# The opening stages of an encoder block: engine order written out, tiles cast one ahead, sums evacuated one late, every second stage backwards

## The chip, the cores and the metric

The kernel runs on one core of one Trainium2 chip. The metric is the device time of one execution in microseconds (us). Before the change the median of three runs was 1933.44 us (1930.73 to 1934.36). About 0.2% (4 us) is what a measurement of this kernel can tell from no change.

## The reference, cut to what matters

One layer over a sequence of 256 tokens with 2048 channels, all in float32: a feed-forward half-step, a mixer of two recurrent kinds of heads, and a second feed-forward half-step. Each of the three sublayers reads `x` normalised and then scaled and shifted by a vector that is computed from a conditioning vector `c` ("adaLN"). The change lies in the first sublayer.

```python
mod = (jax.nn.silu(c) @ w_ada + b_ada).reshape(B, 3, 3, D_MODEL)
shift, scale, gate = mod[:, :, 0], mod[:, :, 1], mod[:, :, 2]
def modulate(h, s):
    return _layer_norm(h) * (1.0 + scale[:, s]) + shift[:, s]
g, v = jnp.split(modulate(x, 0) @ w13, 2, axis=-1)      # 2048 x 2*5632
y = (jax.nn.silu(g) * v) @ w2                           # 5632 x 2048
x = _layer_norm(ALPHA * x + 0.5 * gate[:, 0] * y, ln_g, ln_b)
```

## The kernel before, in words

**Products.** Every float32 product is made of three fast ones: an operand is split into a rounded high part and the rest, and high x high, high x low and low x high are summed in PSUM. For a weight tile of 128x2048 that means one load (SyncE's queue), one rounding copy on ScalarE into `hi` (L93) and one subtraction on VectorE into `lo` (L95); `load_w` (L98) does the three. The tiles `raw` have four buffers in all, `hi` and `lo` three each.

**The adaLN vectors.** Each tile of `w_ada` (1 MB, same `raw` buffers) gives 128 elements of a shift, scale or gate vector: VectorE multiplies it by the row of silu(c), which stands in all partitions (`scb`), and sums along it (`ada_tile`, L167). A fraction of such a tile rides along with each weight tile: `tick` (L184) adds a rate to a credit and issues one adaLN tile per whole credit. `ada_until` (L179) issues what is needed now.

**The ramp** (`ramp`, L646). The first 24 blocks of 128 hidden channels of the first sublayer are computed in five stages over the 16 channel blocks of the input (`STAGES` = 2, 3, 3, 4, 4), so that TensorE can start as soon as two adaLN pairs are known. In each stage the loops run over b = 0..5 and p = 0, 1 (gate or value half): twelve pairs (b, p). A pair has two sums of 128 tokens x 512 columns, one PSUM bank each, and 6 products for each channel block of the stage, 1152 in all. The banks are eight. The pair b = 3 keeps its four banks through all stages (`KEPT`); the others are added to a running sum in SBUF after each stage (L726 to L732: in stage 0 copies, most on ScalarE and some on VectorE, then VectorE adds). Before the last pair or the last but one of a stage, `modulate` (L206) prepares the next stage: transposes on TensorE, scale and shift on ScalarE (L217), rounding (L220), the rest on VectorE (L221); `ahead` is the next stage's first weight tile. In stage 0 the pairs of `EARLY` begin with channel block 0 alone.

**What sets the order.** Where code calls an engine through `V`, `A`, `G`, `T` (L123, `Pinned`), its instructions stay in program order among themselves. All others (`nc.vector`, `nc.scalar`, `nc.tensor`, `nc.sync`) are put in an order by the framework's scheduler, which also gives a new tile whichever buffer comes free. In the ramp before, nearly all casts, sums and evacuations are of the second kind; only the opening (`A.copy`, `V.tensor_sub` in L691 to L700) is pinned. After the ramp `g2(0)` (L760) follows with products `py`.

Of the kernel before, what the change touches and what calls it, by code (L numbers as in the profile page):

```python
# [16 lines left out]
P = 128  # L17
# [32 lines left out]
def block_kernel(ctx: ExitStack, tc: tile.TileContext, a: dict, out: bass.AP):  # L50
# [35 lines left out]
    def split(tile, act, low):  # L86

        raw, name, into = tile
        hi, lo = into() if into else [wp.tile([P, 2048], F32R, tag=w, bufs=3, name=w[0] + name) for w in ("hi", "lo")]
        step = 512 if fine[0] else 2048  # L90
        cols = [slice(c, c + step) for c in range(0, 2048, step)]
        for w in cols:
            act.copy(cut(hi, w), like(raw[:, w], hi))  # L93
        for w in cols:
            low.tensor_sub(cut(lo, w), like(raw[:, w], lo), cut(hi, w).bitcast(F32))  # L95
# [68 lines left out]

    todo = list(enumerate(_ada_tiles()))

    def ada_tile(vec=nc.vector, parts=1):  # L167
        i, (s, j, kt) = todo.pop(0)
        raw = raw_tile(f"ada{i}")
        nc.sync.dma_start(raw, a["w_ada"][i])  # L170
        base = badac[:, s, j, kt:kt + 1]
        for n in range(parts):
            c = slice(n * D // parts, (n + 1) * D // parts)

            to = adac[:, s, j, kt:kt + 1] if n == parts - 1 else sc[:, n:n + 1]
            vec.tensor_tensor_reduce(raw[:, c], raw[:, c], scb[:, c], 1.0, base, ALU.mult, ALU.add, to)  # L176
            base = to

    def ada_until(s, j, kt):  # L179

# [25 lines left out]
    def modulate(s, ns, k0, k, act=nc.scalar, vec=nc.vector):  # L206

        for kt in range(k0, k0 + k, 2):
            w = min(2, k0 + k - kt)
            ps = bank(f"tu{s}_{kt}")  # L210
            for j in range(w):
                for t in range(NT):
                    nc.tensor.transpose(ps[:, j * S + t * P:j * S + (t + 1) * P],
                                        ns[t][:, (kt + j) * P:(kt + j + 1) * P], ident)
            u = sm.tile([P, 2, S], F32, tag="u", bufs=2, name=f"u{s}_{kt}")
            for j in range(w):
                act.activation(u[:, j, :], ps[:, j * S:(j + 1) * S], AF.Identity,  # L217
                                     bias=modc[:, s, 0, kt + j:kt + j + 1],
                                     scale=modc[:, s, 1, kt + j:kt + j + 1])
            act.copy(uh[:, kt:kt + w, :], u[:, 0:w, :])  # L220
            vec.tensor_sub(ul[:, kt:kt + w, :], u[:, 0:w, :], uh[:, kt:kt + w, :].bitcast(F32))  # L221
# [357 lines left out]
    def ffn(s, w13, w2, start, following=None):  # L579
# [65 lines left out]

        def ramp(ns):  # L646

            kept = {}
            n_w = k0 = 0
            ns, rest = ns()  # L650
            for st, k in enumerate(STAGES):
# [5 lines left out]
                held = {}  # L657
                hls = {} if first else {0: ahead}

                def tile_of(i):  # L660
                    if i not in hls:
                        hls[i] = load_w(a["w13_r"][n_w + i], f"ra{n_w + i}")
                    return hls[i]

                def banks(b, p):
                    if b == KEPT:
                        if first:
                            kept[p] = [bank(f"k{'gv'[p]}{t}") for t in range(NT)]
                        return kept[p]
                    return [bank(f"r{'gv'[p]}{st}_{b}{t}") for t in range(NT)]  # L670

                def products(b, p, pss, j0, j1):

                    for t in range(NT):
                        tk = slice(t * P, (t + 1) * P)
                        for j in range(j0, j1):
                            i = (2 * b + p) * k + j
                            hi, lo = tile_of(i // 4)
                            w = slice(i % 4 * 512, (i % 4 + 1) * 512)
                            go = j == 0 and (first or b != KEPT)  # L680
                            end = j == k - 1 and (last or b != KEPT)
                            nc.tensor.matmul(pss[t], uh[:, k0 + j, tk], hi[:, w], start=go, stop=False)
                            nc.tensor.matmul(pss[t], uh[:, k0 + j, tk], lo[:, w], start=False, stop=False)  # L683
                            mm = nc.tensor.matmul(pss[t], ul[:, k0 + j, tk], hi[:, w], start=False, stop=end)  # L684
                    return mm

                if first:


                    credit[1] = 0.0  # L690
                    ada_tile(V, 2)  # L691
                    ada_tile(V)
                    raw, _, _ = load(a["w13_r"][0], "ra0")
                    hi, lo = hls[0] = [wp.tile([P, 2048], F32R, tag=w, bufs=3, name=w[0] + "ra0") for w in ("hi", "lo")]
                    for i in (0, 2, 1, 3):
                        w = slice(i * 512, (i + 1) * 512)
                        A.copy(hi[:, w], raw[:, w])
                        V.tensor_sub(lo[:, w], raw[:, w], hi[:, w].bitcast(F32))
                        if i == 0:
                            modulate(0, ns, 0, 1, A, V)  # L700
                    for n, (b, p) in enumerate(EARLY):
                        held[b, p] = banks(b, p)
                        products(b, p, held[b, p], 0, 1)
                        if n == 0:
                            rest()
                    with tc.issue_after(V.last.ins):
                        ada_until(0, 1, 1)
                    credit[:] = 0.0, RAMP_RATE[0]
                    modulate(0, ns, 1, 1)
                for b in range(RAMP // 4):  # L710
                    for p in range(2):

                        if b == RAMP // 4 - 1 and p == (k > 2) and not last:
                            k1 = k0 + k
                            tile_of(3 * k - 1)
                            ahead = load_w(a["w13_r"][n_w + 3 * k], f"ra{n_w + 3 * k}")
                            ada_until(0, 1, k1 + STAGES[st + 1] - 1)
                            modulate(0, ns, k1, STAGES[st + 1])
                        if (b, p) in held:
                            pss = held[b, p]  # L720
                            end = products(b, p, pss, 1, k)
                        else:
                            pss = banks(b, p)
                            end = products(b, p, pss, 0, k)
                        if b != KEPT:
                            for t in range(NT):  # L726
                                if first and p and t:
                                    nc.vector.tensor_copy(part[b, p][t], pss[t])
                                elif first:
                                    nc.scalar.copy(part[b, p][t], pss[t])  # L730
                                else:
                                    nc.vector.tensor_add(part[b, p][t], part[b, p][t], pss[t])  # L732
                        turn_one(end)
                    if last and b < 4:
                        g, v = (kept if b == KEPT else {p: part[b, p] for p in range(2)}).values()
                        for t in range(NT):
                            swiglu(b, t, g[t], v[t])
                n_w += 3 * k
                k0 += k

        def g1(gi):
            grp = groups[gi]
# [461 lines left out]
def _layout(x, c, w_ada, b_ada, ffn1_w13, ffn1_w2, w_in, b_in, mlstm_norm_g, rg_conv_w, rg_conv_b, rg_wa, rg_ba,  # L1204
# [5 lines left out]
    o["w_ada"] = np.stack([w[t] for t in _ada_tiles()])  # L1210
    o["b_ada"] = _chan(b_ada[0])
    for i, (w13, w2) in enumerate(((ffn1_w13, ffn1_w2), (ffn2_w13, ffn2_w2)), 1):

# [4 lines left out]

    w = ffn1_w13[0].reshape(KT, P, 2, NFF // 4, 512)[:, :, :, :RAMP // 4]
    k0, tiles = 0, []  # L1220
    for k in STAGES:
        tiles.append(w[k0:k0 + k].transpose(1, 3, 2, 0, 4).reshape(P, -1, 2048).transpose(1, 0, 2))
        k0 += k
    o["w13_r"] = np.ascontiguousarray(np.concatenate(tiles))
    w, b = w_in[0], b_in[0]
# [37 lines left out]
```

## Time and profile before

| | |
|---|---|
| Median of three runs | 1933.44 us (1930.73 to 1934.36) |
| The profiled execution, its own time | 1936.85 us |
| Its span from first to last instruction | 1934.9 us |
| TensorE busy | 1892.8 us, 98% of the span |
| VectorE, ScalarE busy | 1429.8 us (74%), 841.1 us (43%) |
| Moved from HBM | 509.22 MB, 264 GB/s over the span |

In the views, PE is TensorE's matmuls, PEld its weight loads, DVE VectorE, ACT ScalarE, POOL GpSimd, SP SyncE (SPq: its DMA issues). PEclk is the clock that TensorE was granted, as a share of full speed. A name such as `rra` is the raw weight tile of the ramp, `hra` and `lra` its two parts; `rg` and `rv` the sums for gate and value half, `kg` and `kv` those that keep their banks; `yacc`, `gate` and `x` are the places in SBUF where the others are added up; `tu` the transposed input, `u` the modulated one; `ada` a tile of `w_ada`. A matmul's record lasts longer than its spacing, since they are pipelined. Lines that begin with a start time are from a timeline: start, duration, engine, line, operation; in brackets the idle time before it and what ended that.

### The profile page before, as it was taken

Reading aid. Unit: us, or ns where it says so; the run is one execution under the profiler, and the core shown is the slowest. Engines: PE = TensorE matmul, PEld = TensorE weight load, DVE = VectorE, ACT = ScalarE, POOL = GpSimd, SP = SyncE. Lnnn points to the kernel's source line nnn. Section 1 sums busy time; section 2 is a strip of 40 time slices with the busy share of each in tenths; the row PEclk is TensorE's granted clock in tenths of the full one; section 3 lists DMA queues with packets and bytes.
Section 4 is the critical chain, followed back from the end, with each engine's and each line's share of the span. In section 5 each row is a group of like instructions: output and inputs, shape, how many; then the busy total and the mean of one; then the engine's idle time right before and its main releaser. Section 6 shows DMA issues by size and latency. Waiting matters only on the chain.

```text
span 1934.9 us, 21428 instructions
## 1 busy us (share of the span) xinstructions
PE 1892.8 (98%) x8680; PEld 1562.4 (81%) x8680; DVE 1429.8 (74%) x1381; ACT 841.1 (43%) x808; POOL 35.3 (2%) x59
## 2 busy tenths in 40 slices
PE   6999999999999999999999999999999999999997
PEld 5878788888888888788888886888888888888885
DVE  7999898887877988798987886655656644445656
ACT  5434344533334335757543346533444334333350
POOL 0000000000000000000000121000000000000000
PEclk8999999999999999999999999999999999999999
DMA  8998878998888787477787674666666655554562
GB/s 349 350 345 328 324 284 328 348 347 323 325 318 334 293 338 287 147 292 263 255 310 283 229 290 177 239 225 254 246 253 250 230 194 196 187 187 177 191 226 77
DMA packets 72675, 512.71 MB, mean 265 GB/s; under 512 B 8448, under 2 KB 8576, under 8 KB 10880
## 3 DMA queue, kind: packets, MB, share of 16 engines
q1 hardware_dynamic: 70848, 507.54, 70.4%
q10 hardware_dynamic: 1728, 3.80, 0.5%
q8 instruction: 68, 1.11, 0.2%
q14 instruction: 31, 0.25, 0.0%
HBM read 509.22 MB, written 2.10 MB: 264 GB/s over the span
## 4 chain that ended last, share of the span: by engine, by line
PE 89%; DVE 5%; issue 3%; DMA 2%; ACT 1%; POOL 0%; DVEq 0%; ACTq 0%; POOLq 0%
PE pj L249 6%; PE py L259 6%; PE py L261 6%; PE py L260 6%; PE fg L259 6%; PE fg L261 6%; PE fg L260 6%; PE fv L260 6%; PE fv L261 6%; PE fv L259 6%; PE pj L250 3%; PE tl L260 2%; PE tl L261 2%; PE tl L259 2%; PE rg L683 2%
## 5 line engine op out<-in xcount | busy, mean ns | idle before, releaser
L176 DVE CUSTOM_DVE_ANT_0 ada<-ada,scb,badac 128x2048 f32<-128x2048 f32 x142 | 333.5, 2351 | 60.1 <-DMA ada<-in_w_ada 59.8
L95 DVE TENSOR_TENSOR lw<-rw,hw 128x2048 fp32r<-128x2048 f32 x80 | 183.3, 2291 | 107.5 <-ACT hw L93 107.5
L93 ACT CAST hw<-rw 128x2048 fp32r<-128x2048 f32 x80 | 153.1, 1914 | 242.6 <-PE py L261 119.7
L95 DVE TENSOR_TENSOR lfv<-rfv,hfv 128x2048 fp32r<-128x2048 f32 x60 | 137.5, 2292 | 129.3 <-ACT hfv L93 129.3
L95 DVE TENSOR_TENSOR lfg<-rfg,hfg 128x2048 fp32r<-128x2048 f32 x60 | 137.5, 2291 | 97.2 <-ACT hfg L93 97.2
L93 ACT CAST hfg<-rfg 128x2048 fp32r<-128x2048 f32 x60 | 114.9, 1915 | 198.1 <-PE fv L261 74.1
L259 PE MATMUL py<-hw,hth 128*128 128x512 f32 x512 | 200.1, 392 | 0.0
L261 PE MATMUL py<-hw,htl 128*128 128x512 f32 x512 | 199.4, 389 | 0.0
L260 PE MATMUL py<-lw,hth 128*128 128x512 f32 x512 | 199.1, 389 | 0.0
L93 ACT CAST hfv<-rfv 128x2048 fp32r<-128x2048 f32 x60 | 114.8, 1913 | 179.8 <-PE fg L261 137.3
L259 PE MATMUL fg<-hfg,u 128*128 128x512 f32 x480 | 187.8, 392 | 0.0
L261 PE MATMUL fg<-hfg,u 128*128 128x512 f32 x480 | 186.9, 389 | 0.0
L260 PE MATMUL fv<-lfv,u 128*128 128x512 f32 x480 | 186.7, 389 | 0.0
L261 PE MATMUL fv<-hfv,u 128*128 128x512 f32 x480 | 186.7, 389 | 0.0
L260 PE MATMUL fg<-lfg,u 128*128 128x512 f32 x480 | 186.7, 389 | 0.0
L259 PE MATMUL fv<-hfv,u 128*128 128x512 f32 x480 | 186.6, 389 | 0.0
L249 PE MATMUL pj<-u,hs 128*128 128x512 f32 x512 | 181.3, 399 | 0.0
L93 ACT CAST hra<-rra 128x2048 fp32r<-128x2048 f32 x47 | 89.9, 1914 | 136.5 <-PE rv L684 48.9
L250 PE MATMUL pj<-u,ls 128*128 128x256 f32 x512 | 143.8, 281 | 0.0
L249 PEld LDWEIGHTS pj<-u,hs 128*128 128x128 f32 x512 | 96.1, 188 | 23.4
L95 DVE TENSOR_TENSOR lra<-rra,hra 128x2048 fp32r<-128x2048 f32 x47 | 107.4, 2287 | 7.9 <-ACT hra L93 7.9
L261 PEld LDWEIGHTS py<-hw,htl 128*128 128x128 f32 x512 | 96.1, 188 | 20.2
(449 smaller groups left out, 3593.0 us busy)
## 6 DMA issues: line engine op xcount, KB each, us to landing
ada<-in_w_ada SPq DMA_DIRECT2D x144, 1024.0 KB, 5.0
rw<-in_w SPq DMA_DIRECT2D x80, 1024.0 KB, 4.9
rfg<-in_w SPq DMA_DIRECT2D x60, 1024.0 KB, 4.9
rfv<-in_w SPq DMA_DIRECT2D x60, 1024.0 KB, 4.9
rra<-in_w_r SPq DMA_DIRECT2D x48, 1024.0 KB, 5.7
rs<-in_w_s SPq DMA_DIRECT2D x32, 1024.0 KB, 5.0
rwo<-in_w_out SPq DMA_DIRECT2D x16, 1024.0 KB, 4.8
rv<-in_w_vo SPq DMA_DIRECT2D x8, 1024.0 KB, 4.8
```

The lines of the kernel that those rows point to most:

```text
L93: act.copy(cut(hi, w), like(raw[:, w], hi))
L95: low.tensor_sub(cut(lo, w), like(raw[:, w], lo), cut(hi, w).bitcast(F32))
L176: vec.tensor_tensor_reduce(raw[:, c], raw[:, c], scb[:, c], 1.0, base, ALU.mult, ALU.add, to)
L249: nc.tensor.matmul(ps, hi[:, w], u2[:, k].rearrange("p w b -> p (w b)"), start=k == 0, stop=False)
L250: nc.tensor.matmul(ps[:, 0:S], lo[:, w], uh[:, k, :], start=False, stop=k == KT - 1)
L259: nc.tensor.matmul(o, acth[:, k0 + j, tk], cut(hi, w), start=first and j == 0, stop=False)
L260: nc.tensor.matmul(o, acth[:, k0 + j, tk], cut(lo, w), start=False, stop=False)
L261: end = nc.tensor.matmul(o, actl[:, k0 + j, tk], cut(hi, w), start=False, stop=last and j == 3)
L683: nc.tensor.matmul(pss[t], uh[:, k0 + j, tk], lo[:, w], start=False, stop=False)
```

## The change

Five things change, all of them in the ramp.

- The ramp's tiles are cast by `A` and `V`, in program order, and adaLN sums go to `V` (`ordered`). At each pair the casts are issued for the tile that it needs and one tile more.
- A pair's sums are evacuated during the next pair (`pending`, `evacuate`), the first time by a ScalarE copy, later by a VectorE add.
- The pairs of every second stage run backwards (`_pairs`), and the last pair of a stage, which is the first of the next, keeps its banks (`carried`). The weight tiles in HBM are laid out in this order (`_pieces`).
- The opening is written out (`first_stage`): the first adaLN tile (a shift) is stored transposed and summed by TensorE, 16 products with one column each; the first tiles are loaded in halves, and the first weight tile's first quarter ahead of the scale; three pairs begin with channel block 0 instead of two.
- The rates at which adaLN tiles ride along change in stages 0 to 2.

```diff
-EARLY = ((0, 0), (0, 1))
-
-RAMP_RATE = (1.0, 0.67, 0.89, 0.67, 0.75)
+EARLY = ((0, 0), (0, 1), (1, 0))
+def _pairs(st):
+    out = [(b, p) for b in range(RAMP // 4) for p in range(2)]
+    return out[::-1] if st % 2 else out
+def _pieces(st):
+    head = [(*e, j) for j in range(STAGES[st]) for e in EARLY] if st == 0 else []
+    return head + [(b, p, j) for b, p in _pairs(st) for j in range(STAGES[st]) if (b, p, j) not in head]
+RAMP_RATE = (1.5, 0.78, 0.78, 0.67, 0.75)
...
+    ordered = [nc.scalar, nc.vector]
...
-        return split(load(src, name, into), nc.scalar, nc.vector)
+        return split(load(src, name, into), *ordered)
...
+    def ada_tile():
+        for _ in ada_sum(ada_load(), ordered[1]):
+            pass
...
+            ordered[:] = A, V
...
+            def evacuate():
+                if not pending:
+                    return
+                b, p, pss, to_h = pending.pop()
+                if b != KEPT:
+                    for t in range(NT):
+                        if (b, p) in written:
+                            V.tensor_add(part[b, p][t], part[b, p][t], pss[t])
+                        else:
+                            A.copy(part[b, p][t], pss[t])
+                    written.add((b, p))
...
+            def first_stage(ps, tile_of, products, banks, hls, held):
+                shift = ada_load(2)
+                raw = raw_tile("rra0")
+                nc.sync.dma_start(raw[:, 0:512], a["w13_r"][0, :, 0:512])
+                scale = ada_load(2)
+                nc.sync.dma_start(raw[:, 512:], a["w13_r"][0, :, 512:])
+                more = [ada_load(2) for _ in range(2)]
...
+                pa = bank("pa")
+                for kt in range(KT):
+                    T.matmul(pa[:, 0:1], shift[0][:, kt * P:(kt + 1) * P], sc[:, kt:kt + 1],
+                             start=kt == 0, stop=kt == KT - 1)
...
+                for _ in ada_sum(scale, V, 2):
+                    pass
+                high(0)
+                A.activation(adac[:, 0, 0, 0:1], pa[:, 0:1], AF.Identity, bias=badac[:, 0, 0, 0:1])
+                u_low = u_of(0)
+                low(0)
+                u_low()
+                for i in (1, 2, 3):
+                    high(i)
+                steps = chain(*(ada_sum(t, V, 2) for t in more))
+                low(1)
+                next(steps)
+                low(2)
+                for _ in steps:
+                    pass
+                for b, p in EARLY:
+                    held[b, p] = banks(b, p)
+                    products(b, p, held[b, p], 0, 1)
+                u_low = u_of(1)
+                low(3)
+                u_low()
...
+                tile_of(1)
+                fine[0] = False
+                credit[:] = -RAMP_RATE[0], RAMP_RATE[0]
+                tile_of(2)
+                rest()
...
+                    goes_on = not first and (b == KEPT or (b, p) == pairs[0])
+                    stays = not last and (b == KEPT or (b, p) == pairs[-1])
...
+                for b, p in pairs:
+                    need = max(pieces.index((b, p, j)) for j in range(k)) // 4
+                    for i in range(min(need + 2, n_tiles)):
+                        tile_of(i)
+                    if need == n_tiles - 1 and not new_u:
+
+                        ahead = load_w(a["w13_r"][n_w + n_tiles], f"ra{n_w + n_tiles}")
+                        evacuate()
+                        for kt in range(k0 + k, k0 + k + STAGES[st + 1], 2):
+                            w = min(2, k0 + k + STAGES[st + 1] - kt)
+                            ada_until(0, 1, kt + w - 1)
+                            modulate(0, ns, kt, w, A, V)
+                        new_u = True
+                    evacuate()
...
+                    if not last and (b, p) == pairs[-1]:
+                        carried = (b, p), pss
+                    else:
+                        pending.append((b, p, pss, last and b < 4))
+                    turn_one(end)
```

More of the change, by code (lines that the diff above doesn't have):

```diff
@@ L646, in ramp @@
         def ramp(ns):
-            kept = {}
+            kept, written, pending, carried = {}, set(), [], None
             n_w = k0 = 0
+            ordered[:] = A, V
             ns, rest = ns()
+            ahead = None
+            def evacuate():
[9 more added lines that the diff above has]
+                    written.add((b, p))
+                if to_h and p:
+                    g, v = (kept if b == KEPT else {p: part[b, p] for p in range(2)}).values()
+                    for t in range(NT):
+                        swiglu(b, t, g[t], v[t])
@@ L656, in ramp @@
                     new_h(1)
-                held = {}
+                pairs, pieces, n_tiles = _pairs(st), _pieces(st), 3 * k
+                held = {} if first else {carried[0]: carried[1]}
                 hls = {} if first else {0: ahead}
@@ L676, in products @@
                         for j in range(j0, j1):
-                            i = (2 * b + p) * k + j
+                            i = pieces.index((b, p, j))
                             hi, lo = tile_of(i // 4)
                             w = slice(i % 4 * 512, (i % 4 + 1) * 512)
-                            go = j == 0 and (first or b != KEPT)
-                            end = j == k - 1 and (last or b != KEPT)
+                            go = j == 0 and not goes_on
+                            end = j == k - 1 and not stays
                             nc.tensor.matmul(pss[t], uh[:, k0 + j, tk], hi[:, w], start=go, stop=False)
@@ L687, in ramp @@
                 if first:
[L690 to L737, printed above, removed]
@@ L738, in ramp @@
-                n_w += 3 * k
+                    first_stage(bank("tu0"), tile_of, products, banks, hls, held)
+                new_u = last
+                for b, p in pairs:
[11 more added lines that the diff above has]
+                    evacuate()
+                    if (b, p) in held:
+                        pss = held[b, p]
+                        end = products(b, p, pss, 1 if first else 0, k)
+                    else:
+                        pss = banks(b, p)
+                        end = products(b, p, pss, 0, k)
+                    if not last and (b, p) == pairs[-1]:
+                        carried = (b, p), pss
+                    else:
+                        pending.append((b, p, pss, last and b < 4))
+                    turn_one(end)
@@ L1220, in _layout @@
     k0, tiles = 0, []
-    for k in STAGES:
-        tiles.append(w[k0:k0 + k].transpose(1, 3, 2, 0, 4).reshape(P, -1, 2048).transpose(1, 0, 2))
+    for st, k in enumerate(STAGES):
+        tiles.append(np.stack([w[k0 + j, :, p, b] for b, p, j in _pieces(st)]).reshape(-1, 4, P, 512).transpose(
+            0, 2, 1, 3).reshape(-1, P, 2048))
         k0 += k
```

37 lines of the change are left out of this document (32 added, 5 removed).

## The prediction, made before the changed kernel ran

> **What bounds the kernel now.** I read the page first: who is busy, and at what clock.
>
> ```profile
> PE 1892.8 (98%) x8680; PEld 1562.4 (81%) x8680; DVE 1429.8 (74%) x1381; ACT 841.1 (43%) x808; POOL 35.3 (2%) x59
> PE   6999999999999999999999999999999999999997
> PEclk8999999999999999999999999999999999999999
> ```
>
> TensorE sets the time; only the first slice shows a gap and a lower clock. So I cut the ramp where TensorE's idle times lie (windows view; columns: window, its length, busy time of PE, PEld, DVE, ACT, POOL with counts, granted clock, DMA share, GB/s).
>
> ```profile
> 18.79:24.53 5.74, 5.73 (x14) 4.12 (x14) 5.64 (x7) 5.07 (x5) 0.00 (x0) 0.53 0.97 405
> 24.53:26.89 2.36, 0.01 (x1) 0.01 (x1) 2.36 (x3) 0.97 (x2) 0.00 (x0) 1.00 0.99 399
> 26.89:34.47 7.58, 5.53 (x16) 4.09 (x16) 4.40 (x6) 3.46 (x4) 0.00 (x0) 0.77 0.89 369
> 34.47:37.62 3.15, 3.15 (x7) 2.48 (x8) 2.22 (x2) 0.61 (x2) 0.00 (x0) 0.50 0.66 218
> 37.62:59.04 21.42, 20.75 (x93) 16.68 (x91) 17.20 (x13) 12.66 (x15) 0.00 (x0) 0.99 0.91 357
> 107.40:125.16 17.76, 15.68 (x71) 12.12 (x69) 17.50 (x17) 7.92 (x8) 0.00 (x0) 1.00 0.85 325
> 125.16:227.67 102.51, 102.38 (x454) 84.27 (x455) 93.75 (x82) 37.24 (x24) 0.00 (x0) 1.00 0.89 334
> 227.67:236.05 8.38, 5.43 (x21) 4.27 (x20) 8.38 (x7) 4.76 (x7) 0.00 (x0) 0.80 0.78 271
> 307.66:1934.90 1627.24, 1607.40 (x7433) 1328.97 (x7431) 1152.58 (x1121) 707.60 (x682) 33.00 (x48) 0.99 0.68 253
> ```
>
> Ramp and 1152 products lie between 18.79 and 307.66 us. TensorE idles there for 0.01 + 2.35 + 2.05 + 0.67 = 5.1 us up to 59.04 and 2.08 + 0.13 + 2.95 = 5.2 us later. Half clock costs more: length times missing clock is 2.7 + 1.7 + 1.6 + 0.2 = 6.2 us up to 59.04 and 0.20 x 8.38 = 1.7 us at 228 to 236. So 18 us can be had in the ramp. Behind it TensorE works 1607.40 of 1627.24 us: what the ramp gives or loses reaches the end nearly whole. The waits name the places:
>
> ```profile
> PE rg L682 <- ACT u L118: 4.3, 1, 4.3
> PE rv L682 <- ACT u L217: 3.0, 1, 3.0
> PE rg L682 <- ACT u L220: 2.4, 1, 2.4
> PE rg L683 <- DVE lra L95: 2.1, 1, 2.1
> PE rg L682 <- DVE yacc L732: 1.1, 1, 1.1
> PE rv L682 <- DVE x L732: 0.9, 1, 0.9
> PE rg L682 <- ACT u L217: 0.7, 1, 0.7
> ```
>
> The first is the wait for the first product. The second, third and last are waits for a modulated input, 2.1 us one for a low part, and 1.1 + 0.9 us waits for a bank that VectorE had still to empty.
>
> **Prices.** Timelines give spacings, which count where work queues up:
>
> ```profile
> 299.73 0.39 PE L683 MATMUL rg<-lra,u 128*128 128x512 f32 x1
> 307.43 0.39 PE L684 MATMUL rv<-hra,u 128*128 128x512 f32 x1
> 226.17 2.35 DVE L176 CUSTOM_DVE_ANT_0 ada<-ada,scb,badac 128x2048 f32<-128x2048 f32 x1 [1.91 <-DMA ada<-in_w_ada]
> 228.45 2.29 DVE L95 TENSOR_TENSOR lra<-rra,hra 128x2048 fp32r<-128x2048 f32 x1
> 230.65 1.28 DVE L732 TENSOR_TENSOR x<-x,rg 128x512 f32<-128x512 f32 x2
> 231.85 2.28 DVE L95 TENSOR_TENSOR lra<-rra,hra 128x2048 fp32r<-128x2048 f32 x1
> 227.82 0.71 PE L213 MATMUL tu<-ident,n 128*128 128x128 f32 x5
> L213 PE MATMUL tu<-ident,n x32: 270/272/473, 11.5 to 228.3; 128*128 128x128 f32 x32
> ```
>
> Between the two products lie 34 steps (33 products stand between them): 7.70 / 34 = 0.2265 us each. A low part takes VectorE 230.65 - 228.45 = 2.20 us, an adaLN sum 2.28 with its read-out, an add 1.20 / 2 = 0.60, and five transposes whose single records last 0.27 at the least are over in 0.71: (0.71 - 0.27) / 4 = 0.11 us each.
>
> **Part 1, the opening and stage 0.** Before, the first product hangs on the first weight tile:
>
> ```profile
> 5.40 6.25 PE L142 MATMUL pc<-ident,sc 128*128 128x128 f32 x32 [5.40 <-ACT sc L149]
> 13.83 1.28 DVE L118 CUSTOM_DVE_ANT_0 ada<-ada,scb,sc 128x1024 f32<-128x1024 f32 x1
> 17.22 0.62 ACT L118 CAST hra<-rra 128x512 fp32r<-128x512 f32 x1 [3.27 <-DMA rra<-in_w_r]
> 17.75 0.56 ACT L118 ACTIVATE u<-tu,adac 128x256 f32<-128x256 f32 x1
> 18.79 0.79 PE L682 MATMUL rg<-hra,u 128*128 128x512 f32 x1 [4.32 <-ACT u L118]
> 6.56:9.79 3.23, 3.23 (x17) 3.23 (x16) 3.19 (x7) 1.19 (x3) 0.23 (x1) 1.00 0.97 389
> 10.30:13.71 3.41, 1.46 (x12) 1.23 (x11) 2.99 (x6) 2.61 (x7) 0.86 (x3) 1.00 1.01 425
> 12.27:17.24 4.97, 0.47 (x1) 0.18 (x1) 4.72 (x5) 1.03 (x5) 0.63 (x2) 0.67 1.01 427
> DMA to landing us min/median/max: 4.8/6.2/12.2
> ```
>
> The weight tile is the fifth megabyte on the queue (two of `x`, two adaLN tiles, itself) and lands at 17.2 at 427 GB/s, 2.46 us for each (the last row is the ramp's weight loads, issue to landing: at least 4.8 us). In the new order the scale ends after 4.25 MB, so at 15.4; its second half is summed by 16.7. TensorE's half: the shift's halves land at 11.0 and 12.3. Sixteen float32 products are 32 records, as `pc` shows; at `pc`'s 6.25 / 32 = 0.195 us they end at 11.65 + 6.25 = 17.9, at the 1.46 / 12 = 0.12 us of the window at full clock at 12.3 + 16 x 0.12 = 14.2. That clock held until 13.7, so I take some 18 of them fast and 14 slow: 16.5, and with four transposes 17.4; `u` needs both this and the scale. From the start of `u` to the first product it is 1.04 us as now: 18.4 (17.8 to 19.8). Next late is channel block 1: ScalarE's quarter cast, then on VectorE two quarters at 0.6 and four half sums at 1.28, then `u`: 18.4 + 0.5 + 6.3 + 1.0 = 26.2. The 18 early products (4.1 us of work) fill 7.8 us, whatever the clock: 3.7 lost. From there 126 products need 28.5 us and up to 1.7 for a slow start: 56.4. VectorE's list from 26.2 is 1.0 + 2.4 (tile 1) + 5 x 2.20 + 6 adaLN x 2.28 = 28.1: 54.3 without any wait, and now in fixed order. It will wait for casts, which ScalarE issues behind `rest()` and 18 copies. I take stage 1's first product at 60. Now: at 59.04 TensorE had done 40.25 - 11.3 = 28.9 of stage 0's 144 x 0.2265 + 1.1 = 33.7 us, so the same point stands at 63.9. **-3.9 us**, with ends -7.5 (56.4) and +0.5. The upper end is this: if tile 1 gets the first weight tile's buffer and not the scale's, its load waits for the last quarter's subtraction at 26.8, lands 4.8 us later and costs some 4.4 us.
>
> The loads in halves put more issues on SP's queue, where the transfers (427 GB/s, back to back) and not the issues are the limit; if halves run like `x`'s 512 KB pieces (389 GB/s), the scale lands 0.5 us later, inside the ends. The Trainium skill speaks against halves: "DMA: Bandwidth & Descriptors", Bandwidth, wants transfers of at least 1 MiB and gives 341 GB/s for a 1 MB transfer. At no more than that the scale's sum would come 1.4 us later (an estimate), 0.7 us past TensorE's half, and the forecast would be 1924.9; in the trace pieces of 512 KB that queue up ran at 389.
>
> **Part 2, stages 1 and 2.** VectorE's work in stage 2 was 9 x 2.20 + 8 adaLN (0.89 x 9) x 2.28 + 20 x 0.60 + 1.2 = 51.2 us against TensorE's 216 x 0.2265 + 0.9 = 49.8: hence full VectorE and lost 2.08 + 0.13 us at 107 to 168. Now 7 sums (0.78 x 9) and 18 adds, since the carried pair isn't evacuated: 19.8 + 16.0 + 10.8 + 1.2 = 47.8. Stage 1, which gets the seventh sum and has 16 adds (one pair's first copies fall to ScalarE): 46.6 against 49.6. Both fit. **-2.2 us** (0 to -2.2); next late would be TensorE itself.
>
> **Part 3, the end of stage 3.** Here `u` waited:
>
> ```profile
> 227.69 1.91 ACT L93 CAST hra<-rra 128x2048 fp32r<-128x2048 f32 x1 [3.53 <-PE rg L684]
> 229.51 1.92 ACT L217 ACTIVATE u<-tu,adac 128x256 f32<-128x256 f32 x4
> 231.48 0.47 PE L682 MATMUL rv<-hra,u 128*128 128x512 f32 x1 [2.95 <-ACT u L217]
> ```
>
> `rv` is the last pair of stage 3. Kept banks 4, the pair before 2, `tu` 2: it waits until `u` empties a `tu` bank, and `u` stands behind a cast that itself waited for TensorE to free a `hi` buffer. Cast one ahead, that cast has its buffer a pair earlier (a pair is a tile here, 24 products, 5.4 us). So `u` starts with the transposes, and the pair's banks come from two adds. **-4.6 us** (2.95 idle and 1.7 of half clock; 0 if the add stands behind another 2.2 us instruction). The Trainium skill, "TensorE: Matmul & The Clock Gate", Why this matters for your kernels, has idle gaps up to about 3 us keep the clock. By that the term is -2.95 and the forecast 1925.9; the trace disagrees: after 2.36 and 2.95 us of idle the clock fell to 0.77 and 0.80.
>
> **Part 4, what the fixed order adds.** VectorE's add for a pair now stands behind the next tile's adaLN sum and low part, ScalarE's copies and `u` behind a cast; behind a waiting instruction queue all later ones, and TensorE waits for banks. The trace of before has no such order. Nearest rows: a boundary or bank wait that is not the big one costs 0.7 to 1.1 us. Bounds: 0, and 4.6 at each of four boundaries, 18.4. I take **+1.5**, two such waits, because a pair lasts 4.1 us or more and the add needs 1.2.
>
> Layout and reversal remove and add no product and no byte: nothing. Sum: -3.9 - 2.2 - 4.6 + 1.5 = -9.2. The profiled execution took 1936.85 us, 3.41 above the median of the runs: 1927.65 there, **1924.2** as a median.
>
> **Rivals.** *A, slower: VectorE's order.* Slack for each tile is (49.6 - 46.6) / 9 = 0.33 us in stage 1, 0.22 in stage 2, 0.79 in stage 3 (12 tiles; 288 x 0.2265 + 0.9 = 66.1 against 26.4 + 8 x 2.28 + 18 x 0.60 + 1.2 = 56.6) and 0.21 in stage 4 (65.2 + 32 transposes = 68.7 against 26.4 + 18.2 + 20 adds and 16 steps of the gated product at 0.60 = 66.2). If each low part waits w for its cast with the adds behind it, stages 1, 2 and 4 lose 30 w - 7.5 us. From w = 0.53 that eats the 8.5 us of parts 1 and 3; at 0.8 it is 16.5, and the time 1933.4 - 8.5 + 16.5 = 1941. For it: VectorE was full. Against:
>
> ```profile
> DVE lra L95 <- ACT hra L93: 7.9, 6, 2.7
> ```
>
> 7.9 us over 47 tiles is 0.17 each, and ScalarE has room.
>
> *B, no change:* stage 0 at its late end (+0.5), `u` still late at the end of stage 3, only part 2 left: -1.7, 1931.7. For it: `u` still stands behind `ahead`'s cast in program order. *C, half:* as B in stage 0, but part 3 holds: 0.5 - 2.2 - 4.6 + 1.5 = -4.8, 1928.6.
>
> **Numbers.** Forecast 0.58, C 0.17, B 0.13, A 0.12. Within 0.2% (4 us, what a measurement of this kernel can tell) are B and a good third of C: 0.20; slower 0.12; faster 0.68. Range: below, parts 1 to 3 at their best and part 4 nil, -14.3: 1919; above, past C and B to 1934, leaving out most of A.
>
> **What would show it.** First product near 18.4; stage 1's near 60; no wait of PE for L732 near 107 to 125; no gap of 3 us near 225 and clock 1.00 from about 40 us on; `py` from about 298.5 instead of 307.66. Wrong if VectorE's waits for `hra` pass 20 us, or PE waits for adds at stage ends.

## The result, and the profile after

| | before | after |
|---|---|---|
| Median | 1932.09 us (1930.63 to 1934.36, 4 runs) | 1962.73 us (1961.66 to 1965.35, 4 runs) |
| Profiled execution, its span | 1936.85 us, 1934.9 us | 1965.35 us, 1963.2 us |

The ratio is 1.0159, interval 1.0146 to 1.0172: slower by some 30 us, where 9.2 us less was forecast. One execution of `e1_evac_first`, a kernel of the experiments below, took 2463.41 us at a granted clock of 0.727; that kernel's figures leave it out. The page of the changed kernel, to be set against the first rows of the prediction (busy time; TensorE and its clock in 40 slices of 49 us):

```profile
PE 1905.3 (97%) x8712; PEld 1570.8 (80%) x8712; DVE 1422.3 (72%) x1373; ACT 844.5 (43%) x817; POOL 35.3 (2%) x59
PE   7899988999999999999999999999999999999997
PEclk8999998999999999999999999999999999999998
```

The first slice is better than before (7 for 6). The second (49 to 98 us), the sixth and the seventh (245 to 344 us) stand at 8 where all were 9, and in the seventh the clock dips too. Cut at the gaps (windows view of the changed kernel; columns as in the prediction, PE's busy time second):

```profile
18.21:53.80 35.59, 32.17 (x126) 24.92 (x126) 28.30 (x29) 22.44 (x29) 0.00 (x0) 0.91 0.94 357
53.80:60.08 6.28, 0.01 (x2) 0.00 (x1) 5.13 (x6) 2.44 (x3) 0.00 (x0) 0.87 0.95 382
60.08:109.06 48.98, 48.98 (x204) 39.98 (x204) 40.66 (x34) 20.20 (x18) 0.00 (x0) 0.95 0.84 322
109.06:114.22 5.16, 1.03 (x6) 0.62 (x6) 4.32 (x5) 2.84 (x4) 0.00 (x0) 0.89 0.94 357
114.22:166.10 51.88, 51.88 (x216) 42.38 (x216) 43.69 (x40) 16.80 (x11) 0.00 (x0) 0.94 0.76 282
166.10:171.57 5.47, 1.29 (x10) 0.84 (x9) 4.36 (x5) 2.84 (x4) 0.00 (x0) 0.96 0.97 367
171.57:268.00 96.43, 96.43 (x425) 79.77 (x426) 80.47 (x70) 37.40 (x29) 0.00 (x0) 0.98 0.79 296
268.00:330.00 62.00, 50.50 (x210) 39.29 (x208) 43.52 (x44) 22.80 (x23) 0.00 (x0) 0.89 0.55 208
329.43:1963.20 1633.77, 1611.93 (x7455) 1332.05 (x7453) 1163.81 (x1133) 709.30 (x683) 32.98 (x48) 1.00 0.69 255
```

Idle time plus length times missing clock, counted as the prediction did for before:

| Stretch | idle | half clock | lost |
|---|---|---|---|
| opening and most of stage 0 (to 53.80) | 3.4 | 0.09 x 35.59 = 3.2 | 6.6 |
| before stage 0's last two pairs | 6.3 | 0.05 x 48.98 = 2.4 | 8.7 |
| before stage 1's last two pairs | 4.1 | 0.06 x 51.88 = 3.1 | 7.2 |
| before stage 2's last two pairs | 4.2 | 0.02 x 96.43 = 1.9 | 6.1 |
| last stage | 11.5 | 0.11 x 62.00 = 6.8 | 18.3 |

With a wait of 1.6 us just behind them this is 48.5 us; before it was 18.2 (5.1 + 5.2 idle, 6.2 + 1.7 clock). The difference is 30.3. The ramp grew by 28.9 (the spans' 28.3, and its first product came 0.58 earlier), which is the same as nearly as a clock of two digits allows. Behind the ramp nothing changed: of the last row's 1633.77 us, 22 records of the ramp (5.0) and the 1.6 are still the ramp's, and 1627.2 are left, as before. So the ramp lost it all, and the last stage most. What ended TensorE's waits (18 to 337 us):

```profile
PE rg L796 <- ACT x L135: 6.3, 1, 6.3
PE rg L796 <- ACT u L135: 5.6, 3, 3.6
PE rg L797 <- DVE lra L135: 3.7, 2, 2.7
PE rv L796 <- ACT u L135: 3.6, 1, 3.6
PE kv L797 <- DVE lra L135: 2.7, 1, 2.7
PE kv L796 <- ACT hra L135: 2.2, 1, 2.2
PE rg L796 <- ACT hra L135: 2.0, 1, 2.0
```

ScalarE's evacuating copies (`x`) and its `u` hold the boundaries; in the last stage casts and low parts do. Those two engines have time to spare (busy 43% and 72%), so the next question is what they stood at. VectorE's waits in the same stretch, and those of the DMA queue (L100 loads weight tiles, L189 adaLN tiles; `adac` is the column that an adaLN sum writes):

```profile
DVE lra L135 <- ACT hra L135: 28.6, 20, 4.5
DVE htl L662 <- ACT hth L661: 20.8, 6, 6.3
...
SPq L100 <- DVE adac L135: 105.6, 27, 11.2
SPq L100 <- DVE lra L135: 83.5, 21, 8.8
SPq L189 <- DVE lra L135: 61.0, 27, 5.6
SPq L189 <- DVE adac L135: 28.9, 11, 5.8
```

49.4 us of VectorE's time go to two waits, and loads wait for buffers that VectorE has yet to read. Two places show how. The last stage (timelines of VectorE, ScalarE, TensorE; `th`, `hth`, `htl` are the transposed hidden blocks and their two parts, of `turn_one`):

```profile
290.89 0.69 DVE L662 TENSOR_TENSOR htl<-th,hth 128x512 fp32r<-128x512 f32 x1 [5.01 <-ACT hth L661]
291.50 2.34 DVE L135 CUSTOM_DVE_ANT_0 ada<-ada,scb,badac 128x2048 f32<-128x2048 f32 x1
293.76 2.29 DVE L135 TENSOR_TENSOR lra<-rra,hra 128x2048 fp32r<-128x2048 f32 x1
...
290.27 0.58 ACT L661 CAST hth<-th 128x512 fp32r<-128x512 f32 x1 [4.33 <-PE th L659]
290.75 1.90 ACT L135 CAST hra<-rra 128x2048 fp32r<-128x2048 f32 x1
...
292.71 0.73 PE L796 MATMUL kv<-hra,u 128*128 128x512 f32 x2 [2.24 <-ACT hra L135]
296.10 0.79 PE L797 MATMUL kv<-lra,u 128*128 128x512 f32 x1 [2.66 <-DVE lra L135]
```

ScalarE's next cast starts right behind `hth` and shows no wait of its own. It stood behind `hth`, which had waited 4.33 us for TensorE's transposes, and these come at the end of a pair. VectorE likewise: the adaLN sum and the low part start right behind `htl`. `turn_one` isn't pinned, and the scheduler put it ahead of pinned work of the next pair. The other place is the end of stage 0:

```profile
57.64 1.90 ACT L135 CAST hra<-rra 128x2048 fp32r<-128x2048 f32 x1 [5.12 <-DMA rra<-in_w_r]
59.45 1.07 ACT L135 COPY x<-rv 128x512 f32<-128x512 f32 x2
...
60.08 0.79 PE L796 MATMUL rg<-hra,u 128*128 128x512 f32 x1 [6.28 <-ACT x L135]
```

The copies that free the next pair's banks stand behind `ahead`'s cast, and that waits 5.12 us for its load. At the ends of stages 1 and 2 it is `u` that stands behind the same cast (3.6 us of TensorE's time each).

### The profile page after: what moved, and what is told of

Same layout as the page of the kernel before. It is cut to its first block, busy times and chain, and to the rows that moved or that the text cites. A ratio compares the mean times of both kernels' runs of the same rounds, so it can differ in the third digit from the quotient of the medians.

```text
span 1963.2 us, 21508 instructions
## 1 busy us (share of the span) xinstructions
PE 1905.3 (97%) x8712; PEld 1570.8 (80%) x8712; DVE 1422.3 (72%) x1373; ACT 844.5 (43%) x817; POOL 35.3 (2%) x59
## 4 chain that ended last, share of the span: by engine, by line
PE 83%; DVE 7%; issue 3%; DMA 3%; ACT 2%; POOL 0%; DVEq 0%; ACTq 0%; POOLq 0%
PE py L288 6%; PE py L289 6%; PE py L287 6%; PE fg L289 6%; PE fg L287 6%; PE fg L288 6%; PE fv L287 6%; PE fv L289 6%; PE fv L288 6%; PE pj L277 5%; PE pj L278 3%; PE tl L288 2%; PE tl L289 2%; PE tl L287 2%; PE o L135 2%
## 5 line engine op out<-in xcount | busy, mean ns | idle before, releaser
L199 DVE CUSTOM_DVE_ANT_0 ada<-ada,scb,badac 128x2048 f32<-128x2048 f32 x104 | 244.3, 2350 | 34.8 <-DMA ada<-in_w_ada 34.7
L135 ACT CAST hra<-rra 128x2048 fp32r<-128x2048 f32 (+1 forms) x54 | 92.4, 1722 | 123.2 <-DMA rra<-in_w_r 47.1
L135 DVE TENSOR_TENSOR lra<-rra,hra 128x2048 fp32r<-128x2048 f32 (+1 forms) x54 | 110.5, 2051 | 28.9 <-ACT hra L135 28.6
L288 PEld LDWEIGHTS py<-lw,hth 128*128 128x128 f32 x512 | 96.2, 188 | 21.4 <-DVE lw L112 2.0
```

The source lines that it names most:

```text
L135: self.last = getattr(self.engine, op)(*args, **kw)
L288: nc.tensor.matmul(o, acth[:, k0 + j, tk], cut(lo, w), start=False, stop=False)
```

## The experiments

Theories. ORDER: instructions written behind others that wait, at particular places, cost the time; SUPPLY: the weight tiles come late for want of buffers, wherever instructions stand; VLOAD: VectorE's work is the bound; V-ORDER and A-ORDER: the order of VectorE alone or of ScalarE alone does it; PINNING: a fixed order costs as such, not by its places. All kernels are edits of the changed one. Ratios are to the kernel before, run beside them (1933.25 us for the first four, 1932.47 for the next four, 1932.85 for the last four).

### The order undone in parts

`e1_evac_first`: the evacuation and the modulation ahead of the next stage's first load and cast.

```diff
-                        ahead = load_w(a["w13_r"][n_w + n_tiles], f"ra{n_w + n_tiles}")
                         evacuate()
...
                             modulate(0, ns, kt, w, A, V)
+                        ahead = load_w(a["w13_r"][n_w + n_tiles], f"ra{n_w + n_tiles}")
```

> At the end of each stage the last pair but one's evacuation and the modulation of the next input are put ahead of the cast of the next stage's first tile (the same work, another order on ScalarE and VectorE). Theory ORDER: the gaps of 6.3, 4.1 and 4.2 us at the ends of stages 0 to 2, with the half clock behind them about 22 us in all, come from copies, adds and the modulated input standing behind a cast that waits for its load; they shrink to under 1 us each, and the time falls to 1944 us (1940 to 1948). Rival SUPPLY: four buffers for raw tiles are too few, the load of that tile comes late in any order and TensorE only meets the wait a pair later, at the tile itself: 1955 us (1950 to 1962). Rival VLOAD: VectorE's total of waits on low parts sets the pace: no change, 1961 to 1964 us.

Measured 1955.53 us, 1.0112 (1.0087 to 1.0138): 7.2 us back, and by its number this is SUPPLY's forecast and not ORDER's. By place it is mixed. The gaps at the end of stage 1 shrank to 0.36 and 0.16 us and that of stage 2 to 0.57, as ORDER said, but at the end of stage 0 3.34, 0.90 and 2.34 us came in place of 6.28: there the tile itself is late, as SUPPLY said. The last stage kept its four gaps over 2 us.

`e2_last_free`: the last stage's work given back to the scheduler.

```diff
                 if last:
+                    ordered[:] = nc.scalar, nc.vector
                     new_h(0)
...
-                            V.tensor_add(part[b, p][t], part[b, p][t], pss[t])
+                            ordered[1].tensor_add(part[b, p][t], part[b, p][t], pss[t])
...
-                            A.copy(part[b, p][t], pss[t])
+                            ordered[0].copy(part[b, p][t], pss[t])
```

> In the last stage casts, adaLN sums and evacuations are handed to the scheduler again instead of standing in program order; the four earlier stages stay as in the changed kernel. Theory ORDER: the 11.5 us of gaps and 6.8 us of half clock at 268 to 330 us come from the next tile's cast, sum and low part standing behind the work on transposed h (ScalarE waits 38.7 us for it, VectorE 20.8 us), which isn't pinned; free, the stage runs as before the change: 1944 us (1941 to 1948). SUPPLY: loads are late in the last stage since buffers come free late, whoever orders: 1957 to 1963 us. VLOAD: 1955 to 1963 us.

1941.41 us, 1.0045 (1.0031 to 1.0060): 21 us back, no gap left in the last stage. `e3_both` is both edits.

> Both edits: evacuation and modulation ahead of the next stage's first cast, and the last stage left to the scheduler. ORDER: the losses at stage ends and in the last stage go together, and the gains of the opening (5 us) and of the end of stage 3 (4.6 us) stay: 1924 us (1920 to 1929), faster than the kernel before. SUPPLY: 1945 to 1955 us. VLOAD: above 1950 us.

1939.10 us, 1.0032 (1.0022 to 1.0041): it fell 15 us short of the expectation, and its 23.6 us are less than the two edits' 21.3 + 7.2. So the two places of the first reading are not all of it. `e4_unpinned` keeps only the opening pinned; the pairs' work goes to the scheduler, while cast-ahead, late evacuation, reversal and opening stay.

```diff
                     first_stage(bank("tu0"), tile_of, products, banks, hls, held)
+                    ordered[:] = nc.scalar, nc.vector
...
-                            modulate(0, ns, kt, w, A, V)
+                            modulate(0, ns, kt, w, *ordered)
```

(and the two evacuation lines as above)

> Only the opening keeps its fixed order; from stage 0's pairs on all casts, sums, evacuations and modulations are handed to the scheduler, while reversal, carried pair, one-ahead casts, one-late evacuation, rates and opening stay. ORDER: the pinning is the cause of most of the loss, the scheduler puts the work about as it did before the change: 1926 us (1920 to 1935). A rival REST: what costs is not the pinning but the carried pair, the reversal or the rates, which stay here: 1945 us or more.

1927.45 us, 0.9974 (0.9963 to 0.9984): faster than before. From the same views as of the changed kernel:

```profile
PE rg L796 <- ACT u L135: 2.2, 2, 1.1
...
DVE lra L112 <- ACT hra L110: 4.7, 8, 1.0
...
SPq L100 <- DVE lra L112: 68.5, 26, 5.0
SPq L100 <- DVE adac L199: 61.3, 24, 3.8
SPq L189 <- DVE lra L112: 55.6, 18, 4.8
SPq L189 <- DVE adac L199: 52.5, 19, 4.7
```

Of nearly the same work VectorE waits 4.7 us for the pairs' casts, not 28.6, and no wait for `hth` shows among its waits. The DMA queue tells less: its rows for weight tiles (L100) are 59.3 us less, those for adaLN tiles (L189) 18.2 more. ScalarE's casts of the ramp's weight tiles wait for their loads as long as in the changed kernel (51.7 us in 15 waits; there 47.1 in 12), and TensorE's longest wait is still only 1.1 us. The written order costs 1962.73 - 1927.45 = 35.3 us: ORDER or PINNING, not VLOAD, and not SUPPLY by itself, since the buffers are the same. REST fell too. It is also the version that beats both kernels.

### One engine's order, and one place of it

As `e4_unpinned`, but one engine stays pinned: VectorE in `e5_vector_pinned` (first line), ScalarE in `e6_scalar_pinned` (second).

```diff
+                    ordered[:] = nc.scalar, V
...
+                    ordered[:] = A, nc.vector
```

> From stage 0's pairs on only VectorE's casts, sums, adds and low parts stay in program order; ScalarE's casts, copies and modulation are handed to the scheduler. Theory V-ORDER: VectorE's order alone costs the time, because it waits for a cast or for transposed h with adaLN sums behind it whose tiles have landed, so raw buffers come free late: 1955 to 1963 us, VectorE's waits for casts above 20 us. Theory A-ORDER: ScalarE's order costs it, because copies and modulated inputs stand behind a cast that waits for its load: 1927 to 1935 us, as with both handed over.

> The counterpart: from stage 0's pairs on only ScalarE stays in program order. V-ORDER: 1927 to 1935 us. A-ORDER: 1950 to 1963 us, with the gaps at the ends of stages 0 to 2. If both engines' orders cost a part, both kernels lie between, 1935 to 1950 us.

1959.41 us, 1.0145 (1.0129 to 1.0162), and 1935.62 us, 1.0018 (1.0000 to 1.0037). VectorE's order costs 32 us by itself, ScalarE's 8; together that is more than the 35.3 of both, so the two overlap. VectorE's waits with VectorE pinned:

```profile
DVE htl L662 <- ACT hth L661: 28.4, 6, 7.2
DVE lra L135 <- ACT hra L110: 17.9, 14, 3.5
```

and TensorE's longest wait with ScalarE pinned, the end of stage 0 again:

```profile
PE rg L796 <- ACT x L135: 6.5, 1, 6.5
```

Is it pinning as such? `e7_turn_late` pins more: `turn_one`'s work goes into the same written order, behind the next pair's casts.

```diff
-            nc.scalar.copy(hth[:, i:i + 4, tk], ps)
-            nc.vector.tensor_sub(htl[:, i:i + 4, tk], ps, hth[:, i:i + 4, tk].bitcast(F32))
+            ordered[0].copy(hth[:, i:i + 4, tk], ps)
+            ordered[1].tensor_sub(htl[:, i:i + 4, tk], ps, hth[:, i:i + 4, tk].bitcast(F32))
...
                         tile_of(i)
+                    if end_of:
+                        turn_one(end_of.pop())
...
-                    turn_one(end)
+                    end_of.append(end)
```

> The changed kernel, all of its order kept, but the work on transposed h is pinned too and issued behind the next pair's casts instead of ahead of them. Theory ORDER, for the last stage: it isn't pinning as such that costs 18 us there, but that the next cast, sum and low part stand behind a wait for the pair's end; put ahead, the last stage runs without gaps: 1944 us (1940 to 1948), as with the last stage handed over (1941). Rival PINNING: any written order is worse there than the scheduler's, since no fixed place suits every pair: 1952 to 1963 us.

1946.15 us, 1.0072 (1.0054 to 1.0090): 16.6 us back with more pinned, not less. Of the last stage's gaps one of 1.01 us is left. VectorE's waits:

```profile
DVE lra L135 <- ACT hra L135: 25.2, 18, 4.6
DVE htl L135 <- ACT hth L135: 3.9, 2, 3.0
```

The 20.8 us at `htl` were the ones that counted in the last stage; the 28.6 at casts hardly moved. Of the 22.9 us between the two profiled spans 18.6 lie behind the end of stage 2. The rest lies ahead of it, where the edit changes no order: at the ends of stages 1 and 2 TensorE waits 1.71 and 2.15 us for `u`, not 3.56 and 3.61. No run says why. `e8_no_carry` is `e4_unpinned` without reversal and without the pair that is held over a stage's end.

```diff
-    return out[::-1] if st % 2 else out
+    return out
...
-                held = {} if first else {carried[0]: carried[1]}
+                held = {}
...
-                    goes_on = not first and (b == KEPT or (b, p) == pairs[0])
-                    stays = not last and (b == KEPT or (b, p) == pairs[-1])
+                    goes_on = not first and b == KEPT
+                    stays = not last and b == KEPT
```

> The kernel with its pairs' work handed to the scheduler (1927.5 us), but all stages run forwards and no pair keeps its banks: eight more adds on VectorE (4.8 us) and no pair in common at the stage ends. Prediction's part 2: VectorE's room in stages 1 and 2 is 2 to 3 us, so 1.2 us more in each stage still fits, and the time stays within 1926 to 1930 us. Rival: the carried pair also saves waits at the stage ends, since the first pair of a stage needs no empty banks: 1931 to 1935 us, most of the gain gone.

1928.81 us, 0.9989 (0.9978 to 1.0000): 1.4 us from `e4_unpinned`, less than can be told apart. So reversal and carried pair together neither cost nor gain anything that can be measured here.

### Buffers, both places, and the opening's sum

`e10_slots` is the changed kernel with two more buffers of 1 MB for adaLN tiles behind the opening and in stages 1 and 2, places that stand empty until the last stage.

```diff
-        raw = raw_tile(f"ada{i}")
+        raw = slot(f"ada{i}")[:, 0:D] if roomy[0] else raw_tile(f"ada{i}")
```

> The changed kernel with its full written order; only the adaLN tiles of the opening's tail and of stages 1 and 2 go into two buffers that stand empty until the last stage, so that the weight tiles have the four raw buffers for themselves there. SUPPLY (the idle times at the ends of stages 0 to 2 come from loads that wait for a buffer): the weight tile's load starts earlier, the casts ahead of the evacuating copies don't wait, the gaps of 6.3, 3.6 and 3.6 us near 54, 111 and 168 us shrink to under 1.5 us each, with the half clock behind them; the last stage is as it was. 1962.7 less some 18 = 1945 (1941 to 1950). ORDER (instructions stand behind others that wait, wherever buffers are): the same gaps, VectorE still waits for hra by 20 us or more, 1955 to 1963.

1954.95 us, 1.0109 (1.0095 to 1.0124): by the number at the edge of ORDER's forecast, by place between the two. At the ends of stages 1 and 2 no gap over 0.73 us is left, and VectorE's waits for casts are under ORDER's 20 us; at the end of stage 0 one gap of 4.65 remains. The waits:

```profile
PE rg L800 <- DVE lra L136: 7.3, 2, 4.7
...
DVE htl L663 <- ACT hth L662: 21.0, 6, 6.4
DVE lra L136 <- ACT hra L136: 12.7, 10, 3.5
```

Buffers recover 8 of 35 us and leave the last stage as it was. They nearly end ScalarE's waits for the ramp's loads (4.4 us, not 47.1), so late loads are not where the larger part goes. `e11_slots_unpinned` has the same edit on `e4_unpinned`.

> The kernel whose pairs' work is ordered by the scheduler (1927.45), with the two more buffers of the run above. SUPPLY: TensorE's left-over gaps (at most 1.14 us each) shrink, 1923 to 1925. ORDER: with the order free the supply doesn't bind any more, 1926 to 1929, no difference that can be measured.

1936.51 us, 1.0017 (1.0007 to 1.0027): 9 us slower than without the two buffers, which no theory had. The profiled execution, at 1945.22 us an outlying one, shows this:

```profile
71.38 0.56 ACT L246 ACTIVATE u<-tu,adac 128x256 f32<-128x256 f32 x1 [11.04 <-DVE adac L200]
```

and TensorE's wait behind it, 4.45 us at 72.00. In VectorE's timeline the two sums ahead of it waited 1.87 and 2.61 us for their tiles' loads: the `u` of a new stage hangs on adaLN tiles that came late on the one queue. That more buffers let other loads go ahead of them is argued, not shown. Either way buffers are no cure: with the order free the same four do (`e4_unpinned`). The Trainium skill, "Perfetto Trace Analysis", Optimization Strategy, says that consistent bubbles can mean too little room for the next tile, by buffer count or tile size. The DMA queue's long waits for VectorE here (105.6 us in one row) invite that reading, and yet the cure by buffers gave 8 us, that by order 35.

`e12_order_mended` puts `e7_turn_late` and `e1_evac_first` together, all still in a written order.

> The changed kernel, fully in a written order, with both places mended in it: the transposed h's work pinned behind the next pair's casts, and the evacuation and the modulation ahead of the next stage's first load and cast. ORDER by places (the two edits add up): 1962.7 - 16.6 - 6.9 = 1939 (1936 to 1943), py near 303. PINNING (an order that leaves the scheduler no choice costs more than its places): 1944 or more, with new waits elsewhere, since the moved cast puts the wait on the tile itself.

1938.23 us, 1.0027 (1.0016 to 1.0037): as ORDER said, the places add up (16.6 + 7.9, where 16.6 + 6.9 had been expected). `py` started at 310.85, not near 303; the expected time itself would have put it near 310 (1939, less 1.9 between time and span, less the 1627.2 behind the ramp). 10.8 us remain to `e4_unpinned`. About half of them lie just behind stage 0, where the tile itself is late again (window of this kernel: 4.7 us idle and 0.22 x 10 = 2.2 of half clock; in `e4_unpinned` one gap of 1.1 us stands there):

```profile
60.00:70.00 10.00, 5.33 (x15) 3.33 (x16) 7.17 (x6) 5.37 (x6) 0.00 (x0) 0.78 0.94 364
```

The rest is several waits of 2 us and less. Whether a better written order exists was not tried, so whether PINNING as such has a part in the 10.8 us stays open.

`e9_shift_on_vector` is `e4_unpinned` with the first shift tile summed by VectorE in halves, and not stored transposed.

```diff
-                for kt in range(KT):
-                    T.matmul(pa[:, 0:1], shift[0][:, kt * P:(kt + 1) * P], sc[:, kt:kt + 1],
-                             start=kt == 0, stop=kt == KT - 1)
...
-                for _ in ada_sum(scale, V, 2):
+                for _ in chain(ada_sum(shift, V, 2), ada_sum(scale, V, 2)):
```

> The kernel whose pairs' work is ordered by the scheduler (1927.45), with the first shift tile summed by VectorE in halves, as its scale is, and not by TensorE. By the prediction's sum u waits for the scale's second half, which is summed at 16.7 either way, and VectorE has the 2.6 us for the shift while it waits for loads: first product at 18.0 to 18.5, time 1926.5 to 1928.5, no difference. VLOAD (VectorE's work in the opening sets the first product): first product 2 us or more later, 1929.5 to 1931.

1927.43 us, 0.9972 (0.9962 to 0.9981), first product at 18.39 us for 18.15: TensorE's sum is worth nothing that can be measured. The timelines show why, of this kernel and then of `e4_unpinned`:

```profile
15.95 1.28 DVE L135 CUSTOM_DVE_ANT_0 ada<-ada,scb,adac 128x1024 f32<-128x1024 f32 x1
17.34 0.56 ACT L135 ACTIVATE u<-tu,adac 128x256 f32<-128x256 f32 x1 [1.98 <-DVE adac L135]
```

```profile
15.43 1.28 DVE L135 CUSTOM_DVE_ANT_0 ada<-ada,scb,adac 128x1024 f32<-128x1024 f32 x1
17.10 0.56 ACT L135 ACTIVATE u<-tu,adac 128x256 f32<-128x256 f32 x1 [0.74 <-PE tu L135]
```

The scale is summed at 17.2 us here and at 16.7 there; but there `u` waits for transposes that stand behind TensorE's sum, so of the 0.5 us by which the scale is ready earlier about half is left at the first product.

## Why the prediction was wrong, point by point

- **Part 4 is the step that failed**: "I take +1.5, two such waits", with 18.4 as the upper bound. Measured: 35.3 us, nearly twice that bound. The reason given, that "a pair lasts 4.1 us or more and the add needs 1.2", looked at adds alone, and the bound counted the four stage ends alone; the last stage, where most was lost (18.3 us), had no term. What stood in the queues was longer: a cast that waits 5.12 us for a load, with copies and `u` behind it (7 to 8 us: `e1_evac_first` against the changed kernel, `e12_order_mended` against `e7_turn_late`), and `hth` and `htl`, which wait up to 10.9 and 6.3 us for the end of a pair, with the next cast, sum and low part behind them (16.6 us, `e7_turn_late`). Both mended give 24.5 us (`e12_order_mended`); the other 10.8 are placed only in part. The bound from before's rows failed because before had no written order: a bound from nearest rows needs the wait itself, not the waits that a scheduler had left over.
- **The step had no term for supply.** VectorE waiting at one instruction keeps tiles that have landed in their buffers. Weight loads waited 189 us for buffers here and 130 in `e4_unpinned`, adaLN loads 90 and 108. `e10_slots` nearly ends the casts' waits for loads and gets 8 us. That it was VectorE's standing still that made them late is argued, not shown.
- **Part 1, right for the opening, not for stage 0.** First product 18.21 (forecast 18.4), block 1 at 26.26 (26.2), TensorE's sum over at 16.12 (16.5). Stage 1's first product, at which the term was taken, came at about 68.1, not 60 and past the late end: the gap at the end of stage 0 stands ahead of it. In `e4_unpinned` it came at about 58.0.
- **Part 2, right in kind.** Of the waits for adds in stages 1 and 2 (2.1 us) two of 0.57 are left; the order's waits for `u` (3.6 each) took their place. The carried pair, which was to save adds, gains nothing that can be measured (`e8_no_carry`); the lower rate was not run by itself.
- **Part 3, right.** In the window from 171.57 to 268.00 TensorE has no idle time, where 2.95 us and half clock stood near 228. The prediction's remark that the clock fell after 2.36 us of idle is not in its rows, since ahead of that gap the clock was at 0.53 already; the gap of 2.95 us does show a fall. With parts 1 to 3 and the pairs' order free (`e4_unpinned`) `py` starts at 297.38, where parts 1 to 3 alone make 307.66 - 10.7 = 297.0; the profiled execution gains 1936.85 - 1926.77 = 10.1. That the sum comes so near is in part luck, since `e4_unpinned` is faster in stage 0 than the forecast and no run takes the cast one ahead out alone. The medians give only 5.8, and the ratio's interval 3 to 7: the profiled execution of before lay 3.4 us above the median of its runs, that of `e4_unpinned` 0.7 below. How much of the 10 us is gain and how much is which execution was profiled stays open.
- **Rival A had the sign and the engine, not the place.** Waits for `hra` passed the 20 us that the prediction had named as its refutation. But 28.6 us over 46 whole tiles is 0.62 each, and by its formula 30 x 0.62 - 7.5 = 11.1 us lost against 8.5 gained: 1936, not 1962.7. The largest single part came with `htl`, which A didn't hold. B and C fell.

## What to carry to other kernels

When an edit fixes the order of an engine's queue, list for every instruction in it what it waits for and how long that can last at worst, and count all that stands behind; the trace of the scheduled kernel here showed 7.9 us of waits for casts, that of the written order 28.6, and 20.8 more at `htl`. Mind above all the unpinned work that lands between pinned instructions. If loads seem to come late, see first whether the engine that frees their buffers stands still at something else.

## What the runs showed of the hardware

An operand of one column saves less than its width suggests: TensorE's 32 records for sixteen float32 products of one column took 4.52 us here, at a granted clock of 1.00 up to 13.70 us and of 0.59 behind. In `e2_last_free`, at 1.00 throughout, they took 3.73 us: 0.12 for a record, 0.23 for a product. A step with 512 columns takes 0.2265 (the prediction's spacing), and a product of the ramp is three of these.

```profile
11.60 4.52 PE L135 MATMUL pa<-sc,ada 128*128 128x1 f32 x32
```

A single short gap can cost the clock. In `e12_order_mended` TensorE had run at full clock when it waited 1.89 us; behind that the windows give 0.54 for 3.4 us:

```profile
255.00:261.40 6.40, 6.40 (x31) 5.00 (x29) 6.40 (x8) 4.21 (x3) 0.00 (x0) 1.00 0.88 338
261.43:263.32 1.89, 0.01 (x1) 0.00 (x0) 1.89 (x3) 0.18 (x1) 0.00 (x0) 1.00 0.90 290
263.32:266.70 3.38, 3.38 (x8) 2.61 (x9) 3.34 (x3) 0.63 (x1) 0.00 (x0) 0.54 1.01 422
```

The gap's price was 1.89 + 0.46 x 3.38 = 3.4 us. In `e3_both` a gap of 1.60 us (266.49) left the clock at 1.00. The Trainium skill, "TensorE: Matmul & The Clock Gate", Why this matters for your kernels, asks for no idle gaps over about 3 us; here 1.89 was enough, and the measurement decides.
